# Hybrid decoder layer on one core: norm row spread by TensorE, zero products, later token tiles, one-part reload and paired weight groups

## The chip, the cores and the metric

The kernel runs on one core of one Trainium2 chip. The metric is device time in microseconds of one execution. A core has five engines that run their own instruction streams in order: TensorE (PE, with its weight loads listed apart as PEld), VectorE (DVE), ScalarE (ACT), GpSimd (POOL) and SyncE (SP), which here issues nearly all DMA transfers.

## The reference, cut to what matters

One decoder layer over 2048 tokens of width 1024. The input is RMS-normed once and multiplied by one input projection; its columns feed a gated DeltaNet (four heads, chunkwise) and a differential attention (four heads); both results are gated, concatenated, multiplied by an output projection and added to the input.

```python
def hybrid_mixer(layer_idx, x, cos, sin, w_norm, w_in, conv_w, ...):
    hn = rms_norm(x, w_norm)
    proj = jnp.einsum("bsd,de->bse", hn, w_in.astype(f32))
    q_a, k_a, v_a, z_a, b_a, a_a, q_b, k_b, v_b, z_b = jnp.split(proj, idx, axis=-1)
    qkv = jax.nn.silu(causal_depthwise_conv(jnp.concatenate([q_a, k_a, v_a], -1), conv_w))
    ...
    o_a = gated_delta_rule_chunked(q_a, k_a, v_a, g, beta)
    o_a = rms_norm(o_a, gdn_norm_w) * jax.nn.silu(z_a)
    ...
    o_b = diff_attention(q_b, k_b, v_b, lam)
    o_b = rms_norm(o_b, subln_w, SUBLN_EPS) * (1.0 - lam_init) * jax.nn.silu(z_b)
    return jnp.einsum("bse,ed->bsd", jnp.concatenate([o_a, o_b], -1), w_out)
```

## The kernel before

**Work.** Tokens are taken as 16 tiles of 128. A tile is loaded (`x_load`), squared and summed on ACT, scaled on DVE by its norm factor and by `wnb`, the norm weight spread over 128 partitions (`x_scale`), transposed on PE and split in two parts, `hh` and `hl`, by ACT and DVE (`x_split`). Four tiles make one instance of the pair (`hh`, `hl`), 512 tokens wide; only two instances fit in SBUF at a time.

**Input projection.** The columns of `w_in` are cut into groups of about 256; a group's weights come in two DMA halves (`wr`), are split into `wh` and `wl` (`w_stream`), and every product is three matmuls (wh·hh, wl·hh, wh·hl). There are three passes: pass 0 takes the first 1024 tokens through 8 groups (two gate groups, six DeltaNet groups), pass 1 the other 1024 tokens through all 16 groups, pass 2 the first 1024 tokens through the remaining 8. So instances 0 and 1 serve pass 0, 2 and 3 pass 1, 4 and 5 pass 2. The gate groups are token-major (256 or 264 moving columns, 24 matmuls for a tile), the DeltaNet groups channel-major (512 columns). `in_jobs` lists the jobs: inside a group the first 512 tokens (tb = 0), then the second (tb = 1); at a change of pass the last two groups are taken as a pair, both at tb = 0 and then both at tb = 1, so that the first instance comes free earlier.

**Reload.** Pass 2 needs the instances of pass 0 again. `hx_store` writes their `hh` and `hl` to DRAM, 8 transfers of 1 MB, and `hx_load` reads them back, 8 transfers of 1 MB.

**Order.** The instruction streams are written by a planner, `Flow`. Each part of the work is a generator that yields an engine, an earliest time and a condition; the planner always emits the piece that could start first by its own cost figures, ties broken by a priority. What it writes is then fixed: every engine runs its instructions in that order and waits on semaphores. SP issues its transfers in order too, and eight semaphore slots (`DMAHW0` to `DMAHW7`) are used in turn, so a transfer waits for the one eight places ahead.

**Places that the change touches.** `x_load` issues the tiles; after tile 0 it issues `wnb` as a broadcast read of `w_norm`. `consts` issues two parameter loads early and eleven more once eight tiles have been issued (`XC = 8`), and `w_stream` waits for eight tiles too before it issues the weights of the second group (`XW = 8`). `warm` runs 14 products of zeros on PE at the very start. `epilogue` takes finished products out of the three PSUM buffers `psi`; for gate groups ACT writes an `acc` tile, POOL multiplies it and SP stores it to `za_s`; there are three `acc` tiles. `gdn_a` prepares the DeltaNet blocks (`ssk`, `sv`, `sn`), `gdn_inv` joins the small triangular inverses through `z1`, `z2` and `Tn`.

## Time and profile before

| | us |
|---|---|
| three runs | 1499.89, 1502.4, 1511.44 |
| median of them | 1502.4 |
| the profiled execution | 1505.07 |
| its span, first to last instruction | 1503.3 |

| engine | busy us | share of the span |
|---|---|---|
| PE | 1447.9 | 96% |
| DVE | 954.0 | 63% |
| ACT | 844.4 | 56% |
| POOL | 708.3 | 47% |

The mean granted TensorE clock is 0.991 of its full 2.4 GHz. The profile is one execution. A row of a timeline has the start, the time from first start to last end, the engine, the source line, the operation with output and inputs, and in brackets the idle time before it and what ended it. Lines 81, 140, 152 and 165 are those of helpers that record every operation, so a row is told by its tiles. A matmul row's time contains its latency; successive starts give the rate. A windows row has the stretch, its length, the busy time of PE, PEld, DVE, ACT and POOL with instruction counts, then the granted clock, the DMA engines' busy share and GB/s.

### The profile page before, as it was taken

To read this page: it belongs to the slowest core of one execution; us is meant where nothing else is said; L and a number is where in the kernel's file an instruction comes from. 1 tells how busy PE (TensorE), PEld (TensorE's weight loads), DVE (VectorE), ACT (ScalarE), POOL (GpSimd) and SP (SyncE) were. 2 spreads that over 40 slices of the span, in tenths; PEclk is the share of its full clock that TensorE was granted. 3 is DMA by queue.
4 is the path that set the end of the run, shared out by engine and by line. 5 is a ranking of instruction groups with operands and counts; after the bars stand their busy time and mean duration, and the time that the engine had idled before them with its cause. 6 is when DMAs were issued, how large, how long until landed. Compare 5 with 4: busy or idle time off the path is not lost.

```text
span 1503.3 us, 28117 instructions
## 1 busy us (share of the span) xinstructions
PE 1447.9 (96%) x9959; PEld 1261.3 (84%) x9959; DVE 954.0 (63%) x2644; ACT 844.4 (56%) x1814; POOL 708.3 (47%) x662
## 2 busy tenths in 40 slices
PE   8899998999998999999999999999999999999998
PEld 6888888988778999998899899877887877888787
DVE  6466887569866667772554453217677777888852
ACT  5354464443565553224536543227777998988870
POOL 3411244600433645554452465625665676776661
PEclk9999999999999999999999999999999999999999
DMA  8665648464745665668766449247666454542425
GB/s 206 163 189 197 173 144 163 122 181 102 169 124 163 171 215 174 152 159 236 241 176 178 132 138 221 86 140 249 217 216 219 141 173 137 190 133 92 134 85 178
DMA packets 282893, 250.99 MB, mean 167 GB/s; under 512 B 47313, under 2 KB 252801, under 8 KB 280705
## 3 DMA queue, kind: packets, MB, share of 16 engines
q1 hardware_dynamic: 257408, 236.61, 55.3%
q10 hardware_dynamic: 25344, 12.59, 2.8%
q8 instruction: 79, 1.29, 0.3%
q14 instruction: 62, 0.50, 0.1%
HBM read 156.86 MB, written 92.27 MB: 166 GB/s over the span
## 4 chain that ended last, share of the span: by engine, by line
PE 74%; DMA 7%; DVE 6%; ACT 5%; POOL 4%; issue 2%; SPq 1%; ACTq 0%; POOLq 0%; DVEq 0%
PE psi L140 36%; PE psb L140 17%; PE pss L140 7%; PE psg L140 7%; PE psb L152 3%; ACT p L81 2%; PE psg L152 2%; PE tp L152 2%; DMA wr<-in_w_in_dram 1%; DMA qk_a<-gdx 1%; SPq L165 1%; POOL t L81 1%; DVE p L81 1%; DMA x<-in_x_dram 1%; DMA za_s<-acc 1%
## 5 line engine op out<-in xcount | busy, mean ns | idle before, releaser
L140 PE MATMUL psi<-wh,hh 128*128 128x256 f32 (+1 forms) x1024 | 305.3, 298 | 8.9 <-ACT acc L81 4.5
L140 PE MATMUL psi<-wl,hh 128*128 128x256 f32 (+1 forms) x1024 | 291.4, 285 | 1.3 <-DVE wl L81 1.3
L140 PE MATMUL psi<-wh,hl 128*128 128x256 f32 (+1 forms) x1024 | 290.9, 284 | 0.0
L81 DVE TENSOR_SCALAR_CACHE_REDUCE p<-pss 128x512 f32<-128x512 f32 (+3 forms) x320 | 179.4, 605 | 69.5 <-PE pss L140 66.6
L140 PE MATMUL psi<-hh,wh 128*128 128x512 f32 x512 | 205.8, 402 | 0.0
L140 PEld LDWEIGHTS psi<-wh,hh 128*128 128x128 f32 x1024 | 197.1, 192 | 10.4 <-ACT acc L81 4.9
L140 PE MATMUL psi<-hh,wl 128*128 128x512 f32 x512 | 202.1, 395 | 0.0
L140 PE MATMUL psi<-hl,wh 128*128 128x512 f32 x512 | 201.3, 393 | 0.0
L140 PEld LDWEIGHTS psi<-wl,hh 128*128 128x128 f32 x1024 | 197.4, 193 | 1.7 <-DVE wl L81 1.5
L140 PEld LDWEIGHTS psi<-wh,hl 128*128 128x128 f32 x1024 | 196.6, 192 | 0.0
L81 POOL TENSOR_TENSOR p<-p,p 128x640 f32<-128x640 f32 (+9 forms) x64 | 162.2, 2538 | 62.9 <-ACT p L81 58.1
L81 ACT ACTIVATE p<-p,nm 128x128 f32<-128x128 f32 (+15 forms) x128 | 153.2, 1200 | 20.8 <-DVE p L81 10.8
L81 ACT ACTIVATE raw<-psi 128x512 f32<-128x512 f32 (+1 forms) x96 | 57.2, 596 | 134.5 <-PE psi L140 113.7
L140 PE MATMUL psb<-th,v 128*128 128x256 f32 (+1 forms) x576 | 126.0, 293 | 1.5 <-DVE tl L81 1.2
L140 PE MATMUL pss<-kk,QQ 64*128 64x512 f32 (+3 forms) x960 | 123.2, 382 | 3.7 <-DVE p L81 1.8
L81 DVE SCALAR_TENSOR_TENSOR acc<-raw,cw,acc 128x512 f32<-128x512 f32 x144 | 112.3, 780 | 14.9 <-ACT acc L81 13.3
L81 ACT ACTIVATE p<-p,sc 128x128 f32<-128x128 f32 (+15 forms) x88 | 108.6, 1253 | 18.6 <-DVE sc L81 16.9
L140 PEld LDWEIGHTS psi<-hh,wl 128*128 128x128 f32 x512 | 96.0, 188 | 22.4
L81 DVE TENSOR_TENSOR tl<-psb,th 128x512 fp32r<-128x512 f32 (+2 forms) x176 | 92.9, 563 | 32.3 <-ACT th L81 30.7
L140 PEld LDWEIGHTS psi<-hl,wh 128*128 128x128 f32 x512 | 96.3, 188 | 20.1
L140 PEld LDWEIGHTS psi<-hh,wh 128*128 128x128 f32 x512 | 96.2, 188 | 19.7
L140 PEld LDWEIGHTS pss<-kk,QQ 64*128 64x128 f32 x960 | 80.3, 184 | 36.7 <-issue 9.3
(212 smaller groups left out, 3311.7 us busy)
## 6 DMA issues: line engine op xcount, KB each, us to landing
wr<-in_w_in_dram SPq DMA_DIRECT2D x80, 256.0 KB
x<-gdx SPq DMA_DIRECT2D x32, 512.0 KB
wr<-in_w_in_dram SPq DMA_DIRECT2D x24, 512.0 KB
gdx<-acc ACTq DMA_DIRECT2D x48, 256.0 KB
kk<-qk SPq DMA_DIRECT2D x48, 256.0 KB
v<-v SPq DMA_DIRECT2D x48, 256.0 KB
qk_a<-gdx SPq DMA_DIRECT2D x32, 256.0 KB
qk<-raw SPq DMA_DIRECT2D x32, 256.0 KB
```

The lines of the kernel that those rows point to most:

```text
L81: return call(*args, **kw)
L140: return self.nc.tensor.matmul(out=out, lhsT=lhsT, rhs=rhs, **kw)
L152: return self.nc.tensor.transpose(out=out, in_=in_, identity=identity)
L165: (self.nc.sync if by == "SP" else self.nc.scalar).dma_start(out=out, in_=in_, **kw)
```

## The change

- `w_norm` is loaded as one row of 1024 values; PE multiplies it by a row of ones (two f32 products of 512 columns), and DVE copies the two results to `wnb`.
- After the transposes of tile 0, 12 more products of zeros are issued on PE (`warm2`).
- Tiles 8 to 15 are issued only when three weight groups are done, and they may take one `x5` buffer fewer.
- In `in_jobs` the first two groups of every pass are paired as well, the first two of the program included.
- `hx_store` adds `hh` and `hl` on POOL into an `x5` tile and stores that (8 adds of 128x1024, 8 stores of 512 KB); `hx_load` loads it (4 loads of 1 MB) and splits it again: 4 copies on ACT and 4 subtractions on DVE, each of 128x2048.
- In `gdn_a` a negated `beta` is kept, so that `sn` comes from the reciprocal in one step; `sv` is computed on POOL afterwards.
- In `gdn_inv` the first copy into `z1` moves from ACT to DVE.

```diff
-    hx_s = [[dram.tile([P, KT, TB], F32, name=f"hx{i}_{j}") for j in range(2)] for i in range(2)]
+    hx_s = [dram.tile([P, KT, TB], F32, name=f"hx{i}") for i in range(2)]
...
+    wrow = ga.tile([1, D], F32, name="wrow", tag="fsX")
+    one = ga.tile([1, P], F32, name="one", tag="qk_a", bufs=2)
+    nc.vector.memset(one, 1.0)
+    def w_rows():
+        for i in range(2):
+            yield "PE", (lambda: t_row[0]), lambda: len(t_row) > 0, "+G"
+            ps = ps_g.tile([P, TB], F32, name="psg")
+            mm(out=ps, lhsT=one, rhs=wrow[:, i * TB:(i + 1) * TB], start=True, stop=True)
+            yield DV
+            wnb.append(wk.tile([P, TB], F32, name="wnb", tag=f"t1_{i}"))
+            dve.tensor_copy(out=wnb[i], in_=ps)
+            fl.release("G")
+            t_wn.append(fl.after("DVE"))
...
-                b = x_buf + ([(t_5[0], "ga")] if live5[0] < NX5 else [])
+                b = x_buf + ([(t_5[0], "ga")] if live5[0] < NX5 - (n > 7) else [])
...
-            yield "SP", (lambda: best()[0]), best
+            yield "SP", (lambda: best()[0]), lambda: best() if n < 8 or w_done[0] >= 3 else None
...
-                for i in range(2):
-                    wnb.append(wk.tile([P, TB], F32, name="wnb", tag=f"t1_{i}"))
-                    t_wn.append(dma(out=wnb[i], in_=bcast(w_norm)[:, i * TB:(i + 1) * TB]))
+                t_row.append(dma(out=wrow, in_=w_norm))
...
+    def warm2():
+        yield "PE", NOW, lambda: n_xt[0] > 1, "G"
+        ps = ps_g.tile([P, TB], F32, name="psg")
+        for _ in range(12):
+            fl.op("PE", 215)
+            nc.tensor.matmul(out=ps, lhsT=zw[0][:, :P], rhs=zw[0], start=True, stop=True)
...
-            for kh in range(2):
-                for j in range(2):
-                    yield "SP", NOW, lambda: w_done[0] >= HXW + 3 * (4 * i + 2 * kh + j) // 4
-                    t_hx[i] = dma(out=hx_s[i][j][:, kh * 4:kh * 4 + 4], in_=f(HX[i][j][:, kh * 4:kh * 4 + 4]))
+            for k in range(0, KT, 2):
+                yield "POOL", (lambda: max(*x_ready[i].values(), t_5[0])), (
+                    lambda: all((i, t) in x_done for t in range(4)) and live5[0] < NX5
+                    and w_done[0] >= HXW + 3 * (4 * i + k // 2) // 4)
+                live5[0] += 1
+                t = ga.tile([P, 2, TB], F32, name="x5", bufs=NX5)
+                pool.tensor_tensor(out=t, in0=f(HX[i][0][:, k:k + 2]), in1=f(HX[i][1][:, k:k + 2]), op=ALU.add)
+                yield SP
+                t_hx[i] = dma(out=hx_s[i][:, k:k + 2], in_=t)
...
+            for kh in range(2):
+                k4 = slice(kh * 4, kh * 4 + 4)
+                yield "ACT", (lambda: t_l[kh]), None
+                act.activation(hh[:, k4], hx[:, k4], AF.Copy)
+                yield DV
+                dve.tensor_tensor(out=r(hx[:, k4]), in0=hx[:, k4], in1=f(hh[:, k4]), op=ALU.subtract)
...
-        last = [gi for gi in range(len(groups) - 1) if groups[gi + 1][0] != groups[gi][0]] if SWAP else []
-        return sorted(jobs, key=lambda a: (a[0], 0) if a[0] not in last and a[0] + 1 not in last else
-                      (a[0] + (a[0] + 1 in last) - 1, a[1]))
+        new = [gi for gi in range(len(groups)) if gi == 0 or groups[gi - 1][0] != groups[gi][0]]
+        two = {}
+        for gi in new:
+            for g in (gi, gi - 2):
+                if g >= 0:
+                    two[g] = two[g + 1] = g
+        return sorted(jobs, key=lambda a: (two[a[0]], a[1]) if a[0] in two else (a[0], 0))
...
-            dve.reciprocal(out=sv, in_=ssk)
-            dve.tensor_tensor(out=sv, in0=sv, in1=st["beta"][:, h, cp], op=ALU.mult)
-            dve.tensor_scalar(out=sn, in0=sv, scalar1=-1.0, scalar2=None, op0=ALU.mult)
+            dve.reciprocal(out=sr, in_=ssk)
+            dve.tensor_tensor(out=sn, in0=sr, in1=st["nbeta"][:, h, cp], op=ALU.mult)
...
+            pool.tensor_tensor(out=sv, in0=sr, in1=st["beta"][:, h, cp], op=ALU.mult)
...
-                act.activation(z1[32:64, :, 0], ps[0:32, :, 0:32], AF.Copy)
...
+                dve.tensor_copy(out=z1[32:64, :, 0], in_=ps[0:32, :, 0:32])
```

The instruction order of three places follows. On TensorE, at the start of the kernel before: the last of the warm-up products (`fsT` holds zeros), the eight transposes of tile 0 (`x_180`), then the first products of the projection.

```order
L470 LDWEIGHTS fsT
L470 MATMUL psg<-fsT 128x512
L152 MATMUL tp<-ident,x_180 128x128 x8
L140 MATMUL psi<-wh,hh 128x256
L140 MATMUL psi<-wl,hh 128x256
L140 MATMUL psi<-wh,hl 128x256
```

The same place of the changed kernel, from the last warm-up product to the first of the new products of zeros; tile 0 is `x_183` here.

```order
L487 MATMUL psg<-fsT 128x512
L140 MATMUL psg<-wrow,one 128x512 x2
L152 MATMUL tp<-ident,x_183 128x128 x8
L495 LDWEIGHTS fsT
L495 MATMUL psg<-fsT 128x512
```

The two products that spread the norm row now stand ahead of the transposes, and twelve products of zeros stand behind them; the first projection product comes after those twelve and after four transposes of tile 1.

On TensorE, where the first group ends in the kernel before: `wh_226` and `wl_227` are the weights of the first group, `wh_478` those of the second, `hh_418` and `hl_419` the second instance (tiles 4 to 7), `hh_209` the first (tiles 0 to 3).

```order
L140 MATMUL psi_663<-wh_226,hh_418 128x256
L140 MATMUL psi_663<-wl_227,hh_418 128x256
L140 MATMUL psi_663<-wh_226,hl_419 128x256
L140 MATMUL psi_705<-wh_478,hh_209 128x264
L140 MATMUL psi_705<-wl_479,hh_209 128x264
```

The place in the changed kernel where the second group first appears: `wh_214` and `wl_215` are the first group's weights, `wh_549` and `wl_550` the second's, `hh_217` and `hl_218` the first instance, `x5_296` and `x5_348` tiles 6 and 7.

```order
L140 MATMUL psi_489<-wh_214,hh_217 128x256
L140 MATMUL psi_489<-wl_215,hh_217 128x256
L140 MATMUL psi_489<-wh_214,hl_218 128x256
L152 MATMUL tp_543<-ident_89,x5_296 128x128 x4
L152 MATMUL tp_552<-ident_89,x5_348 128x128 x4
L140 MATMUL psi_568<-wh_549,hh_217 128x264
L140 MATMUL psi_568<-wl_550,hh_217 128x264
L140 MATMUL psi_568<-wh_549,hl_218 128x264
```

The second group's weights are wanted after 96 products of the projection instead of after 192, while the tiles 4 to 7 are wanted only after 192 instead of after 96.

On SyncE, the transfers of the kernel before from tile 6 (`x_283`) and tile 7 (`x_317`) on: the four `wr` rows are the second group's weights, `xt` is tile 8, and the parameters begin with `dtb`.

```order
L165 DMA x_283<-in_x_dram 128x1024
L165 DMA x_317<-in_x_dram 128x1024
L165 DMA wr<-in_w_in_dram 128x4x256
L165 DMA wr<-in_w_in_dram 128x4x8
L165 DMA za_s<-acc_306 128x256
L165 DMA wr<-in_w_in_dram 128x4x256
L165 DMA wr<-in_w_in_dram 128x4x8
L165 DMA xt<-in_x_dram 128x1024
L165 DMA dtb<-in_dt_bias_dram 128x4
```

The end of the same stretch in the changed kernel, behind tile 7 and the first nine parameter loads; the `wr` rows are again the second group's weights.

```order
L165 DMA wqk<-in_q_norm_w_dram 128x64
L165 DMA wqk<-in_k_norm_w_dram 128x64
L348 DMA sub<-in_subln_w_dram 128x1
L165 DMA za_s<-acc_345 128x256
L165 DMA za_s<-acc_401 128x256
L165 DMA wr<-in_w_in_dram 128x4x256
L165 DMA wr<-in_w_in_dram 128x4x8
L165 DMA wr<-in_w_in_dram 128x4x256
L165 DMA wr<-in_w_in_dram 128x4x8
L165 DMA za_s<-acc_487 128x256
```

Eleven parameter loads and two stores now stand ahead of the second group's weights, which stood ahead of them before, and no tile from 8 on is issued in this stretch.

## Rows read from the trace of the kernel before

**Rows 1.** Windows by stage: start, pass 0, turn to pass 1, DeltaNet stretch.

```profile
0.00:79.20 79.20, 66.13 (x463) 60.33 (x464) 42.68 (x70) 35.95 (x87) 29.56 (x46) 0.91 0.71 179
79.20:195.00 115.80, 115.80 (x524) 94.87 (x523) 86.16 (x204) 55.77 (x87) 19.18 (x24) 1.00 0.62 183
195.00:330.00 135.00, 128.98 (x797) 114.92 (x797) 88.62 (x223) 70.98 (x127) 57.70 (x66) 0.97 0.62 156
330.00:900.00 570.00, 549.06 (x4244) 506.12 (x4243) 357.76 (x940) 272.52 (x822) 248.34 (x311) 1.00 0.62 168
...
sum 1503.30, PE 1447.94 PEld 1261.25 DVE 953.99 ACT 844.41 POOL 708.25; mean PE 206.85 PEld 180.18 DVE 136.28 ACT 120.63 POOL 101.18
```

**Rows 2.** Windows where the granted clock (third figure from the right) is low.

```profile
10.00:20.00 10.00, 7.01 (x33) 6.50 (x34) 7.66 (x10) 5.29 (x14) 2.62 (x5) 0.66 0.90 295
48.00:56.00 8.00, 8.00 (x49) 8.00 (x49) 6.71 (x15) 4.64 (x14) 6.31 (x9) 0.67 1.07 249
250.00:260.00 10.00, 7.28 (x40) 6.42 (x39) 5.38 (x17) 4.79 (x7) 5.96 (x8) 0.74 1.06 235
```

**Rows 3.** Waits of TensorE from 0 to 72 us: total, times, longest.

```profile
PE psi L140 <- ACT acc L81: 4.5, 2, 3.4
PE psi L140 <- DVE wh L81: 3.1, 1, 3.1
PE psi L140 <- DVE ab L81: 1.3, 1, 1.3
```

**Rows 4.** Timeline of TensorE, start of the kernel.

```profile
1.36 5.25 PE L470 MATMUL psg<-fsT 128*128 128x512 bf16 x14 [1.36 <-POOL fsT L467]
...
19.58 0.28 PE L140 MATMUL psi<-wh,hh 128*128 128x256 f32 x1
19.70 0.28 PE L140 MATMUL psi<-wl,hh 128*128 128x256 f32 x1
...
27.57 1.08 PE L152 MATMUL tp<-ident,xt 128*128 128x128 f32 x8
28.40 0.36 PE L140 MATMUL psi<-wh,hh 128*128 128x256 f32 x1
...
79.23 0.40 PE L140 MATMUL psi<-hh,wh 128*128 128x512 f32 x1
```

**Rows 5.** Timeline of SyncE's DMA issues, 21 to 42 us.

```profile
21.87 0.98 SPq L165 DMA_DIRECT2D wr<-in_w_in_dram  x2
...
28.66 3.25 SPq L165 DMA_DIRECT2D dtb<-in_dt_bias_dram  x1
...
40.20 1.96 SPq L165 DMA_DIRECT2D za_s<-acc  x3
```

**Rows 6.** Timeline of ScalarE, the longest wait of the start.

```profile
47.10 0.38 ACT L81 ACTIVATE acc<-psi 128x256 f32<-128x256 f32 x1 [5.73 <-DMA za_s<-acc]
```

**Rows 7.** Timeline of VectorE, start of the kernel.

```profile
6.11 1.41 DVE L81 SCALAR_TENSOR_TENSOR x<-x,rsx,wnb 128x512 f32<-128x512 f32 x2 [5.09 <-POOL rsx L81]
...
10.48 0.69 DVE L81 CAST wh<-wr 128x1024 fp32r<-128x1024 f32 x1 [1.55 <-DMA wr<-in_w_in_dram]
11.09 0.68 DVE L81 TENSOR_TENSOR hl<-tp,hh 128x512 fp32r<-128x512 f32 x1
11.69 1.21 DVE L81 TENSOR_TENSOR wl<-wr,wh 128x1024 fp32r<-128x1024 f32 x1
```

**Rows 8.** Timelines of POOL, VectorE and TensorE at the turn to pass 1.

```profile
243.78 2.48 POOL L81 TENSOR_TENSOR wl<-wr,wh 128x1056 fp32r<-128x1056 f32 x1 [0.94 <-ACT wh L81]
...
244.03 2.78 DVE L81 SCALAR_TENSOR_TENSOR x<-x,rsx,wnb 128x512 f32<-128x512 f32 x1
...
255.58 1.12 PE L152 MATMUL tp<-ident,x 128*128 128x128 f32 x4 [2.07 <-DVE hl L81]
```

**Rows 9.** Lines by shape: count, busy us, mean ns, idle before with its releasers.

```profile
L81 DVE TENSOR_TENSOR wl<-wr,wh 128x1024 fp32r<-128x1024 f32 x53 | 69.0, 1301 | 2.8 <-ACT wh L81 1.7
...
L81 ACT ACTIVATE wh<-wr 128x1024 fp32r<-128x1024 f32 x27 | 28.5, 1056 | 8.4 <-DMA wr<-in_w_in_dram 7.5 <-ACT acc L81 0.9
...
L81 POOL TENSOR_TENSOR wl<-wr,wh 128x1024 fp32r<-128x1024 f32 x7 | 17.4, 2489 | 20.1 <-ACT wh L81 20.1
```

More of the change, by code (lines that the diff above doesn't have):

```diff
@@ L433, in hybrid_kernel @@
     xq, x_buf = {}, [(0.0, "wk")] * NXB
+    t_row = []
+    wrow = ga.tile([1, D], F32, name="wrow", tag="fsX")
[11 more added lines that the diff above has]
+            t_wn.append(fl.after("DVE"))
     def x_load():
@@ L467, in warm @@
         nc.gpsimd.memset(z, 0.0)
+        zw.append(z)
         ps = ps_g.tile([P, TB], F32, name="psg")
@@ L470, in warm @@
             nc.tensor.matmul(out=ps, lhsT=z[:, :P], rhs=z, start=True, stop=True)
+    def warm2():
[4 more added lines that the diff above has]
+            nc.tensor.matmul(out=ps, lhsT=zw[0][:, :P], rhs=zw[0], start=True, stop=True)
     N_WARM = 14
+    zw = []
     def x_scale(par, of):
@@ L492, in x_scale @@
             for i in range(2):
-                yield "DVE", (lambda: max(t_r, t_wn[i])), None
+                yield "DVE", (lambda: max(t_r, t_wn[i])), lambda: len(t_wn) > i
                 hs = slice(i * TB, (i + 1) * TB)
@@ L535, in hx_store @@
         for i in range(2):
-            yield "SP", (lambda: max(x_ready[i].values())), lambda: all((i, t) in x_done for t in range(4))
-            for kh in range(2):
-                for j in range(2):
-                    yield "SP", NOW, lambda: w_done[0] >= HXW + 3 * (4 * i + 2 * kh + j) // 4
-                    t_hx[i] = dma(out=hx_s[i][j][:, kh * 4:kh * 4 + 4], in_=f(HX[i][j][:, kh * 4:kh * 4 + 4]))
+            for k in range(0, KT, 2):
[7 more added lines that the diff above has]
+                t_hx[i] = dma(out=hx_s[i][:, k:k + 2], in_=t)
+                live5[0] -= 1
+                t_5[0] = max(t_5[0], t_hx[i])
     t_hx = [0.0] * 2
@@ L548, in hx_load @@
             yield "SP", (lambda: max(t_xu[i + 2], t_hx[i])), lambda: x_used[i + 2]
-            hx = (hn.tile([P, KT, TB], F32, name="hh"), hn.tile([P, KT, TB], F32, name="hl"))
-            HX[i + 4] = tuple(r(h[:, :, :]) for h in hx)
+            hh = hn.tile([P, KT, TB], F32R, name="hh")
+            hx = hn.tile([P, KT, TB], F32, name="hl")
+            t_l = []
             for kh in range(2):
-                for j in range(2):
+                if kh:
                     yield "SP", NOW, None
-                    t = dma(out=hx[j][:, kh * 4:kh * 4 + 4], in_=hx_s[i][j][:, kh * 4:kh * 4 + 4])
+                t_l.append(dma(out=hx[:, kh * 4:kh * 4 + 4], in_=hx_s[i][:, kh * 4:kh * 4 + 4]))
+            for kh in range(2):
[4 more added lines that the diff above has]
+                dve.tensor_tensor(out=r(hx[:, k4]), in0=hx[:, k4], in1=f(hh[:, k4]), op=ALU.subtract)
                 if kh == 0:
-                    x_ready[i + 4] = {n: t for n in range(4)}
-                x_late[i + 4] = t
+                    x_ready[i + 4] = {n: fl.after("PE") for n in range(4)}
+                x_late[i + 4] = fl.after("PE")
+            HX[i + 4] = hh, r(hx[:, :, :])
             x_done.update((i + 4, n) for n in range(4))
@@ L816, in scalars @@
             dve.reciprocal(out=st["beta"], in_=t)
+            dve.tensor_scalar(out=st["nbeta"], in0=st["beta"], scalar1=-1.0, scalar2=None, op0=ALU.mult)
             yield "ACT", None, None
@@ L925, in gdn_a @@
             dve.tensor_scalar(out=ssk, in0=ssk, scalar1=EPS, scalar2=None, op0=ALU.add)
-            dve.reciprocal(out=sv, in_=ssk)
-            dve.tensor_tensor(out=sv, in0=sv, in1=st["beta"][:, h, cp], op=ALU.mult)
-            dve.tensor_scalar(out=sn, in0=sv, scalar1=-1.0, scalar2=None, op0=ALU.mult)
+            sr = ga.tile([P, 2], F32, name=f"sr{par}")
+            dve.reciprocal(out=sr, in_=ssk)
+            dve.tensor_tensor(out=sn, in0=sr, in1=st["nbeta"][:, h, cp], op=ALU.mult)
             yield "DVE", (lambda: t_e), None
@@ L1108, in gdn_inv @@
                 t_z2 = fl.after("PE")
-            if ua is not None:
-                act.activation(z1[32:64, :, 0], ps[0:32, :, 0:32], AF.Copy)
-                t_z1 = fl.after("PE")
             if ue is not None:
@@ L1116, in gdn_inv @@
             if ua is not None:
+                dve.tensor_copy(out=z1[32:64, :, 0], in_=ps[0:32, :, 0:32])
                 dve.tensor_copy(out=z1[96:128, :, 1], in_=ps[32:64, :, 0:32])
-                t_z1 = max(t_z1, fl.after("PE"))
+                t_z1 = fl.after("PE")
             if ub is not None:
@@ L1694, in hybrid_kernel @@
         fl.add(epilogue(par, NE), 0)
+    fl.add(warm2(), 0)
+    fl.add(w_rows(), 0)
     for gen in (q_load(), k_load(), out_x(), v_load()):
```

3 lines of the change are left out of this document (1 added, 2 removed).

## The prediction

> **What bounds the kernel now.** I read the windows by stage first. TensorE is busy 1447.9 of 1503.3 us [rows 1], so it is the bound nearly everywhere, and the change leaves its products as they are. It can only win back TensorE's idle time, 55.4 us in all, and the time lost to a lower clock. The reader is to see where the idle time lies: 13.1 us in the first 79.2 us, none in the rest of pass 0 (115.8 of 115.8 busy), 6.0 at the turn to pass 1, 20.9 in the 570 us in which the DeltaNet chain is woven into the projection [rows 1]. The remaining 15.4 us lie behind 900 us, in parts that the change does not edit.
>
> Second, the windows with a low clock [rows 2]. The granted clock is 0.66, 0.67 and 0.74 in three stretches of 8 to 10 us, which means that TensorE spent about 7 us of each at the lower of its two levels (1.2 GHz). Each such stretch costs about half of that, 3.4 us (0.34 x 10), and each stands during or just behind an idle time of TensorE. Over the first 79.2 us the clock is 0.91, so some 7 us are lost there besides the idle time.
>
> Third, the waits of the start [rows 3]. The two largest are 3.4 us for ACT to empty a `psi` buffer, and 3.1 us for the first `wh`. ACT in turn waited 5.73 us for an `acc` tile to be stored [rows 6], and SyncE tells why: the stores were issued at 40.20, behind parameter loads that began at 28.66 and crept forward for 11.5 us, since each waits for a slot that a 512 KB tile or weight transfer holds [rows 5]. So the middle of the start is bound by the transfer queue, the first 20 us by DVE and the first weights.
>
> **The change part by part.** Durations are those of the profiled execution, so the sum is made against its 1505.1 us, 1.8 more than its span and 2.7 above the median of the three runs.
>
> *Norm row by TensorE.* It removes 512 KB of transfer from in front of the first weights, which were awaited at 10.48 [rows 7], and adds work: two f32 products of 512 columns behind the warm-up, which ends at 6.6 (1.36 + 5.25) [rows 4]. One pass of 256 columns steps at 0.12 us [rows 4], so a pass of 512 takes 0.24 at least; bounds for the two products are 0.5 us at one pass each and some 2 us at several passes each. I take 1.7. DVE then gets its first operand about 7.6 instead of 6.11, and works in order through copy, scale, cast, copy, `wl`, `hl` and scale. By rows of the same width these are 0.7, 0.7, 0.7, 0.7, 1.2, 0.7 and 0.7 us [rows 7]: 5.4 us, so tile 0 is wholly scaled at about 13.0 and transposed at 13.4.
>
> *Zero products.* Twelve of them follow. The 14 of the warm-up took 5.25 us, 0.375 on average [rows 4]. TensorE idles some 3.5 us between 9.5 and 13 while DVE works, as it did in the kernel before ahead of 11.3 us, after which the clock fell [rows 2, 3]. So I price them at the lower clock, 0.43 us each, 5.2 us in all, which makes the first projection product start at 18.6; at the full clock, 0.21 each, it would be 16.0. In exchange what follows should run at full clock.
>
> *Later tiles and the paired first groups.* From 18.6 on TensorE has 384 gate products at 0.12 us, 46.1 us, and the transposes of seven tiles at 0.83 us (28.40 - 27.57) [rows 4], 5.8 us. It can do 96 products and six tiles of transposes, 16.5 us, before the second group begins, that is up to 35. The weights of the second group are issued later than before: then at 21.87 [rows 5], now behind tile 7 (which needs tile 2's buffer, about 22 to 23.5), eleven parameter loads at about 0.5 us each and two stores, so at 28 to 31. With two 512 KB halves, a cast and two subtractions at 1.3 us [rows 9] they are ready between 34 and 39. I take 2.5 us of waiting, bounds 0 and, if the small loads creep as they did before, 11. The wait of 3.4 us for the stores goes, and its 3.4 us of slow clock: tile 8 and those behind it are no longer in the queue, and TensorE can fill six jobs, 17 us (144 x 0.12), before the first store must have landed. Sum: 18.6 + 46.1 + 5.8 + 2.5 + 1 for small waits is 74.0, against 79.2 [rows 4]. The start gives 5 us. With the zero products at full clock and no wait it gives 11; with the second group's weights 10 us later it costs 5.
>
> *Paired groups at the turn.* When pass 1 begins, the first instance is now used for 192 products instead of 96, so TensorE needs tiles 12 to 15 11.5 us later (96 x 0.12). The wait for `hl` of 2.07 us [rows 8] should go, and with it part of the slow clock (0.74 over 10 us [rows 2], of which 2.6 us; the rest of the loss there is that idle time). Against it stands that DVE is the engine that is late there, and its load does not shrink. I take 3 us, bounds 7 and, through the POOL adds below, -2.5.
>
> *One-part reload.* It takes 4 MB of stores and 4 MB of loads away. It adds eight adds on POOL, about 2.49 us each [rows 9], 20 us. POOL is busy 19.2 of 115.8 us there [rows 1], so POOL itself hides them. DVE may not: a DVE scale that takes 0.7 us elsewhere took 2.78 and ended about 0.6 us behind the end of a POOL subtraction of two SBUF operands (243.78 + 2.48) [rows 8]. DVE has 29.6 us idle in pass 0 [rows 1], so I price this at nothing but for one add at the turn, 2.5 us at most. The load adds four copies on ACT, about 2.1 us each, and four subtractions on DVE, about 2.6 us each (twice the rows of 1024 columns [rows 9]). They lie at the turn to pass 2, in front of which TensorE has 96 products of 512 columns, 22 us, with the rest of the DeltaNet chain; a load of 1 MB, a copy and a subtraction fit into that twice.
>
> The Trainium skill (SBUF — State Buffer, SBUF: two separate sides) says that POOL and DVE share one port pair as an exclusive lock held for a whole instruction, the loser fully blocked. The row of 2.78 us agrees. By the rule alone all eight adds could block DVE, and with no slack on DVE the forecast would be 20 us later, near 1514; DVE's idle time in that stretch is why I weigh it at one add.
>
> *Shorter chain in `gdn_a`, join by DVE.* One small DVE instruction fewer in 32 blocks, 32 small copies moved to an engine that is 63% busy there (357.8 of 570 [rows 1]). The gain is what the idle time of 20.9 us allows and what a new order makes of it. I take 1 us, bounds 6 either way.
>
> Sum: 5 + 3 + 1 = 9 us, a profiled execution of 1496 and, 2.7 less, a median of 1494.
>
> **The rivals.** *All waits of the start and the turn clear.* The idle time and clock of both (13.1 + 7 and 6.0 + 3.4) would fall to the unavoidable first 10 us or so, and the gain is 11 + 7 + 2 = 20 us: 1482. For it speaks that each wait named has an edit aimed at it; against it that DVE, the late one at both places, only gets more work there.
>
> *The waits only move.* The planner writes a new order for 900 us, and TensorE runs it blindly; 20.9 us of idle time in the DeltaNet stretch [rows 1] show how far its figures are off. If start and turn give 8 and the new order takes as much, the median stays near 1501.
>
> *Slower: the second group's weights come late.* The place is TensorE's 97th product. If the eleven loads creep for 11.5 us as before [rows 5], the weights are ready near 46 and TensorE stands from 35, with 3.4 us of slow clock behind. Up to there the changed kernel is even until about 40. At 46 the start costs 5 us; with 1.5 lost at the turn and 2 to the rest, 8.5 us: 1511. Against it: fewer large transfers are in flight at that time.
>
> **How the numbers follow.** A measurement of this kernel can tell a change of about 1% from none, 15 us, that is 1487.4 and 1517.4. Forecast, 1488 to 1500: 0.45. All clear, about 1482: 0.27. Only moved, about 1501: 0.17. Slower, about 1511: 0.11. Faster by over 1% are nearly all of the second case and a fifth of the first, 0.35. Slower by over 1% is over half of the last, 0.07, for its price has no firm upper end. Within 1% is 0.58. The range takes the second case with 6 us more on one side and nearly all of the last on the other: 1476 to 1511.
>
> **What would show it.** First channel-major product near 74 instead of 79.2; a product every 0.12 us from about 19 on; no ACT wait on a store; TensorE's wait at the second group's first product 0 to 4 us. At the turn no wait for `hl` over 1 us and a clock of 1.0. POOL adds near 2.5 us. The prediction is wrong if the start does not shorten, if the clock falls again behind the second group, or if TensorE's idle time between 330 and 900 us moves by more than 6 us.

## The result and the profile after

The change makes the kernel slower by 0.7%: 1514.6 us (median of 9 runs, 1510.1 to 1521.6) against 1503.1 us for the kernel before in the same series (9 runs), ratio 1.0072 with a 95% interval of 1.0056 to 1.0088. The forecast was 1494, its range ended at 1511. The kernel before had medians from 1503.1 to 1508.4 us in the series that follow, so all comparisons below are ratios within one series. Stretches and milestones are from one profiled execution each.

Windows by stage of the kernel after, as in [rows 1], cut at its own first channel-major product (84.4 us):

```profile
0.00:84.40 84.40, 71.83 (x480) 61.56 (x481) 35.70 (x63) 30.04 (x67) 22.47 (x37) 0.88 0.52 124
84.40:195.00 110.60, 108.87 (x479) 88.04 (x477) 91.06 (x173) 60.11 (x100) 42.28 (x39) 0.98 0.57 169
195.00:330.00 135.00, 130.93 (x816) 116.63 (x817) 100.08 (x246) 71.23 (x129) 60.08 (x84) 0.99 0.66 165
330.00:900.00 570.00, 545.96 (x4163) 502.10 (x4162) 371.88 (x956) 280.44 (x804) 242.24 (x320) 0.99 0.61 160
```

The start is 5.2 us longer, not 5 shorter; TensorE's idle time in it is no larger (12.6 us against 13.1), its busy time is. Pass 0, which had no idle time of TensorE at all, now has 1.7 us of it up to 195 us and a clock of 0.98. The turn is better: 4.1 us idle instead of 6.0. The DeltaNet stretch is 3.1 us worse (24.0 idle against 20.9).

TensorE's idle time over the whole run hardly moved: 54.0 us (1514.3 - 1460.3) against 55.4. What grew is TensorE's *busy* time, by 12.3 us. The new products are 6.7 of it (4.74 for the zero products, 1.98 for the norm row); the rest, 5.6 us, goes with a lower clock. The windows with a low clock, as in [rows 2]:

```profile
9.00:19.00 10.00, 5.83 (x17) 2.94 (x18) 7.32 (x11) 4.09 (x10) 1.45 (x3) 0.50 0.83 289
40.00:50.00 10.00, 5.01 (x18) 4.20 (x19) 5.00 (x6) 1.08 (x1) 0.00 (x0) 0.65 0.94 128
267.00:274.00 7.00, 6.32 (x42) 6.31 (x42) 6.24 (x18) 2.91 (x5) 5.65 (x7) 0.76 0.22 35
660.00:670.00 10.00, 5.18 (x33) 5.18 (x34) 6.24 (x14) 0.60 (x1) 9.11 (x8) 0.66 0.69 209
780.00:790.00 10.00, 7.79 (x52) 7.33 (x52) 1.39 (x5) 3.34 (x12) 5.73 (x11) 0.66 0.57 168
```

Summed over windows of 5 us, as 5 x (1 - clock) and with the idle parts of those windows counted too, it is 27.2 us against 13.7 before. Each of these windows holds a wait or lies just behind one: 3.77 us up to 14.3, 5.0 us between 40 and 50, 4.8 between 660 and 670. Single waits of over 2 us add up to 20.3 us in the kernel after and to 14.9 in the kernel before. So much the same idle time, with more of it in long waits, goes with twice the slow clock; no run tests by itself whether the longer waits are the cause.

Waits of TensorE from 0 to 80 us, as in [rows 3]:

```profile
PE tp L152 <- DVE x L81: 4.7, 2, 3.8
PE psi L140 <- DVE wl L81: 2.7, 2, 2.0
PE psi L140 <- DVE wh L81: 2.2, 1, 2.2
```

The wait for ACT's `acc` of [rows 3] is gone. The waits for `wh` and `wl` are those for the second group's weights, in TensorE's timeline:

```profile
6.54 1.98 PE L140 MATMUL psg<-wrow,one 1*128 1x512 f32 x4
...
15.19 4.74 PE L495 MATMUL psg<-fsT 128*128 128x512 bf16 x12
...
20.12 0.36 PE L140 MATMUL psi<-wh,hh 128*128 128x256 f32 x1
...
41.37 0.39 PE L140 MATMUL psi<-wh,hh 128*128 128x264 f32 x1 [2.17 <-DVE wh L81]
43.74 0.59 PE L140 MATMUL psi<-wl,hh 128*128 128x264 f32 x1 [1.98 <-DVE wl L81]
47.46 0.59 PE L140 MATMUL psi<-wh,hh 128*128 128x264 f32 x1 [0.94 <-ACT wh L81]
...
48.75 0.59 PE L140 MATMUL psi<-wl,hh 128*128 128x264 f32 x1 [0.70 <-DVE wl L81]
```

Together TensorE waited 5.8 us for these weights.

SyncE's issues show where these weights stood, as in [rows 5], and VectorE's and ScalarE's timelines when they could be used:

```profile
25.32 0.70 SPq L165 DMA_DIRECT2D dtb<-in_dt_bias_dram  x1
...
30.34 0.43 SPq L348 DMA_DIRECT2D sub<-in_subln_w_dram  x1
30.87 0.85 SPq L165 DMA_DIRECT2D za_s<-acc  x2
31.77 4.31 SPq L165 DMA_DIRECT2D wr<-in_w_in_dram  x4
```

```profile
40.61 0.71 DVE L81 CAST wh<-wr 128x1056 fp32r<-128x1056 f32 x1 [2.11 <-DMA wr<-in_w_in_dram]
...
47.44 1.26 DVE L81 TENSOR_TENSOR wl<-wr,wh 128x1056 fp32r<-128x1056 f32 x1 [3.76 <-ACT wh L81]
```

```profile
46.33 1.08 ACT L81 ACTIVATE wh<-wr 128x1056 fp32r<-128x1056 f32 x1 [6.49 <-DMA wr<-in_w_in_dram]
```

The parameter loads did not creep (0.47 us each); the weights went out at 31.8 and still arrived only at 40.6 and 46.3 us. Between 40 and 50 us the DMA engines were 94% busy and moved 128 GB/s (windows above). The kernel before shows the same in two windows that the prediction did not read, with the same weights on the queue (issued from 21.87 on):

```profile
25.00:30.00 5.00, 5.00 (x44) 4.94 (x44) 4.10 (x8) 4.94 (x15) 3.99 (x6) 1.00 1.03 118
30.00:35.00 5.00, 4.42 (x39) 4.22 (x38) 5.00 (x8) 2.23 (x5) 2.75 (x4) 1.00 1.07 105
```

So the slow load (DMA engines full at 105 to 118 GB/s) is not new. New is that these weights are issued 10 us later and that TensorE wants them half a group sooner.

### The profile page after: what moved, and what is told of

It reads as the page before. It is cut to its first block, busy times and chain, and to the rows that moved or that the text cites. A ratio compares the mean times of both kernels' runs of the same rounds, so it can differ in the third digit from the quotient of the medians.

```text
span 1514.3 us, 28218 instructions
## 1 busy us (share of the span) xinstructions
PE 1460.3 (96%) x9975; PEld 1266.9 (84%) x9975; DVE 986.5 (65%) x2653; ACT 853.8 (56%) x1792; POOL 724.1 (48%) x698
## 4 chain that ended last, share of the span: by engine, by line
PE 75%; DVE 9%; DMA 6%; ACT 4%; POOL 3%; issue 2%; SPq 1%; ACTq 0%; DVEq 0%; POOLq 0%
PE psi L140 33%; PE psb L140 18%; PE psg L140 8%; PE pss L140 8%; PE psb L152 4%; DVE acc L81 2%; PE psg L152 2%; PE tp L152 2%; DMA x<-gdx 1%; DMA wr<-in_w_in_dram 1%; DVE wl L81 1%; DMA qk<-acc 1%; POOL rqx L81 1%; POOL t L81 1%; ACT acc L81 1%
## 5 line engine op out<-in xcount | busy, mean ns | idle before, releaser
L81 DVE SCALAR_TENSOR_TENSOR acc<-raw,cw,acc 128x512 f32<-128x512 f32 x144 | 116.1, 810 | 10.5 <-ACT acc L81 9.0
L81 ACT ACTIVATE p<-p,sc 128x384 f32<-128x384 f32 (+15 forms) x89 | 109.6, 1247 | 13.8 <-DVE sc L81 9.3
L140 PE MATMUL psb<-woh,oh 128*128 128x512 f32 x256 | 110.4, 431 | 0.7 <-DVE tl L81 0.6
```

Of the source, the lines that this page charges most:

```text
L81: return call(*args, **kw)
L140: return self.nc.tensor.matmul(out=out, lhsT=lhsT, rhs=rhs, **kw)
```

## The experiments

Sixteen kernels in four sets. "First" is the first channel-major product, "stretch" the time from there to the first product of pass 1. "Kept order" means that the planner counts what was taken out or moved as if it were still there, so that every instruction not named keeps its place; the others are planned anew. Milestones differ from one execution to the next: "after" and the two kept-order kernels that leave the start alone (no POOL adds, join's operand on ACT) have their first channel-major product between 83.0 and 84.7 us.

| kernel | first, us | stretch, us | ratio to before [95%] |
|---|---|---|---|
| before | 79.2 | 148.0 | 1 |
| after | 84.4 | 153.6 | 1.0072 [1.0056, 1.0088] |
| first two groups not paired | 79.3 | 154.9 | 0.9980 [0.9963, 0.9997] |
| second weights ahead of parameters | 84.9 | 154.5 | 1.0203 [1.0174, 1.0232] |
| parameters late | 77.8 | 163.1 | 1.0142 [1.0111, 1.0173] |
| old norm row, no zero products | 78.9 | 155.5 | 1.0023 [1.0006, 1.0040] |
| old reload | 84.0 | 147.5 | 0.9987 [0.9970, 1.0004] |
| planner's DVE constant, on after | 84.9 | 157.0 | 1.0286 [1.0254, 1.0318] |
| planner's DVE constant, on before | 80.9 | 148.0 | 1.0023 [1.0005, 1.0042] |
| planner's ACT constant, on before | 79.8 | 147.6 | 1.0044 [1.0028, 1.0059] |
| turn pairing alone, on before | 80.5 | 147.9 | 1.0153 [1.0123, 1.0182] |
| kept order: second weights first | 80.5 | 154.6 | 1.0043 [1.0028, 1.0058] |
| kept order: no zero products | 83.1 | 154.0 | 1.0065 [1.0048, 1.0082] |
| kept order: no POOL adds | 84.7 | 150.1 | 1.0017 [1.0003, 1.0031] |
| kept order: join's operand on ACT | 83.0 | 154.2 | 1.0077 [1.0055, 1.0099] |
| kept order, before: parameters late | 80.5 | 147.9 | 1.0017 [1.0003, 1.0031] |
| old reload + second weights first | 79.3 | 147.6 | 0.9967 [0.9948, 0.9987] |
| the same, stores between the halves | 78.2 | 147.3 | 0.9932 [0.9914, 0.9951] |

### The start

**First two groups not paired.**

```diff
-        new = [gi for gi in range(len(groups)) if gi == 0 or groups[gi - 1][0] != groups[gi][0]]
+        new = [gi for gi in range(1, len(groups)) if groups[gi - 1][0] != groups[gi][0]]
```

> The changed kernel, but the first two groups are not paired (the pairs at the turns stay). Theory A (the second group's weights come late, and pairing asks for them half a group too early): they are ready near 47 us as in the changed kernel, but are asked for only near 50, so TensorE's 5.0 us of idle time between 40 and 50 go, the first channel-major product comes near 79 instead of 84.4 us, and the median falls by about 5 us, to 1509 or 1510. Rival (the start is late because the zero products put the first projection product at 20 instead of 11 us): first channel-major product still at 83 us or later, median within 2 us of 1514.6. If the order that the planner writes behind it moves the time more than the start does, the median moves by another amount than the first channel-major product does.

The first channel-major product came at 79.3 us, 5.1 earlier, as theory A says. The ratio fell by more, 0.9%, although the POOL adds are still there (stretch 154.9): what lies beyond the start belongs to the new order and was not traced.

**Second group's weights ahead of the parameter loads**, planned anew.

```diff
-            yield "SP", NOW, lambda: n_xl[0] >= XC
+            yield "SP", NOW, lambda: n_xl[0] >= XC and n_w1[0] == 2
```

> The changed kernel with the second group's weights issued before the parameter loads instead of behind them; everything else stays. Theory A: issued at about 25 instead of 31.8 us, the weights are ready near 40, TensorE's idle time between 40 and 50 us falls from 5.0 to about 1, the first channel-major product comes near 79 to 80 us, and the median near 1510. Rival (the 32-byte packets of the gate columns make that load slow wherever it is issued, and the tiles are still under way): ready at 44 or later, first channel-major product at 83 us or later, median unchanged.

A miss. The weights were issued at 24.2 and their second half was cast at 39.2, but TensorE then waited 8.37 us all the same. VectorE's and ScalarE's timelines show what came instead: DVE stood for the last parameter, with the second `wl` behind it in its order, and ACT for a store.

```profile
46.08 0.15 DVE L81 TENSOR_SCALAR sub<-sub 128x1 f32<-128x1 f32 x1 [5.94 <-DMA sub<-in_subln_w_dram]
...
48.23 1.24 DVE L81 TENSOR_TENSOR wl<-wr,wh 128x1056 fp32r<-128x1056 f32 x1
```

```profile
46.43 0.38 ACT L81 ACTIVATE acc<-psi 128x256 f32<-128x256 f32 x1 [5.62 <-DMA za_s<-acc]
```

The start was hardly later than in the changed kernel (84.9 against 84.4), but the median 1.3% worse: that loss lies behind the start, in the new order, and was not traced further.

**Parameters late**, planned anew: the eleven loads and DVE's work on them wait until the first group is done.

```diff
-            yield "SP", NOW, lambda: n_xl[0] >= XC
+            yield "SP", NOW, lambda: n_xl[0] >= XC and w_done[0] >= 1
...
-        yield "DVE", (lambda: t_c + 2000), None
+        yield "DVE", (lambda: t_c + 8000), None
```

> The changed kernel with the eleven parameter loads, and the DVE work on them, put off until the first group's last product is planned; the second group's weights are then issued behind tile 7, and no parameter stands in front of them or of the first stores. The run with the weights moved alone showed them landed by 39 us, and DVE then standing 5.94 us for a parameter and ACT 5.62 us for a store, so the wait had only moved. Theory A: with both out of the way TensorE's idle time between 35 and 50 us falls from 5.0 to 1 or less, the first channel-major product comes near 78 to 79 us, and nothing of it is paid elsewhere. Theory of the order (behind the start, the time moves with each new order): the median is not 5 us below that of the changed kernel, but anything between 1500 and 1525. Rival: the paired start is late for another reason, first channel-major product at 83 or later.

First channel-major product at 77.8, 6.6 us earlier than after; the median is 0.7% worse than after all the same. Both theories held: the start is what theory A says, and the new order took more than it gave.

**The same move in the kept order.** SyncE's calls and DVE's calls on the parameters are put on lists while the planner counts them, and issued at a later place.

```diff
             t_c = dma(out=o, in_=i)
...
+                if gi == 1 and kh == 1:
+                    fl.flush(held[0])
...
+                if gi == 2 and kh == 0:
+                    fl.flush(held[1])
```

> The changed kernel with its order kept instruction for instruction on TensorE, ACT and POOL; only on SyncE the second group's weights go ahead of the eleven parameter loads and two stores, and DVE's eight instructions on the parameters come 9 to 11 places later. The planner does not see it, so nothing is ordered anew. Theory A with the theory of the order: the weights are issued near 25 instead of 31.8 us and ready near 40, TensorE's idle time between 35 and 50 us falls from 5.0 to 1 or less, the first channel-major product comes at 78 to 80 instead of 84.4 us, and since all behind it keeps its order the gain reaches the end: ratio to the kernel before 1.003 to 1.004 instead of 1.0072. The same two moves with a new order behind them gave 1.014. Rival (the pairing itself costs what the run without the pair saved, and a start that is 6 us earlier is lost in waits on DMA and POOL that stand at fixed times): ratio 1.006 or more.

First channel-major product 3.9 us earlier (80.5), and this time the gain lasts: pass 1 begins 2.9 us earlier, the projection ends 5.0 us earlier, the ratio is 1.0043. Of the wait 4.31 us stayed, behind an ACT that stood 2.67 us for a store. So the late weights cost about 4 us of the 11 (1.0072 - 1.0043 = 0.29%; with both intervals, 1 to 8 us).

**No zero products**, kept order.

```diff
-            nc.tensor.matmul(out=ps, lhsT=zw[0][:, :P], rhs=zw[0], start=True, stop=True)
```

> The changed kernel without the 12 zero products; the planner still counts them, so every other instruction keeps its place. If they only delay the first projection product: it comes at about 15.5 instead of 20.1 us, but the second group's weights are still ready only near 47, so TensorE waits longer for them and the first channel-major product stays at 83 to 84.4 us: ratio within 0.002 of 1.0072. If they keep the clock up for what follows (their purpose): the clock between 15 and 30 us falls below 1.0, and the first channel-major product is no earlier or later. If the start is bound by TensorE's own work: first channel-major product near 80, ratio 1.004.

First projection product at 15.8 instead of 20.1, first channel-major product at 83.1, which is within the spread of milestones, ratio unchanged: TensorE waits for the weights instead. The products delay nothing that counts as long as the weights are late. Nor do they raise the clock: from 15 to 30 us it was 0.88 without them and 0.86 with them.

**Old norm row, no zero products**, planned anew (the broadcast is two DMAs again, `w_rows` and `warm2` go).

> The changed kernel with the norm row broadcast by two DMAs as in the kernel before, and without the 12 zero products; the first two groups stay paired. (With these gone the planner also puts the second group's weights before the parameter loads.) If TensorE's broadcast and the zero products are what makes the start late: first projection product near 12 instead of 20.1 us, first channel-major product near 78, median near 1508. If only the late weights count: first channel-major product near 80 because the weights come earlier, and the idle time ahead of them is smaller. If both are harmless and the loss is further on: first channel-major product at 83 or later, median near 1514.

First projection product at 10.9, first channel-major product at 78.9. As the planner also put the weights ahead of the parameters, this alone does not tell the two apart.

**Parameters late in the kernel before**, kept order: SyncE's parameter loads behind three stores and three tiles.

> The kernel before with its order kept instruction for instruction on TensorE, ACT and POOL; on SyncE the eleven parameter loads go behind three stores and three tile loads, and DVE's eight instructions on the parameters come later. The 5.73 us that ACT waited for a store (and TensorE's 3.4 us for a psi buffer, with 1.6 us of slow clock behind) should go. If a gain at the start is kept when the order behind it is kept: first channel-major product near 75 instead of 79.2, ratio 0.997. If the waits behind the start stand at fixed times: first channel-major product early, ratio within 0.001 of 1.000.

A miss: the wait only moved. The third group's weights now stood behind the parameters (issued at 46.27), ACT's cast of them came after its longest wait, and TensorE lost 7.37 us behind it. First ScalarE's row, then TensorE's:

```profile
59.16 1.06 ACT L83 ACTIVATE wh<-wr 128x1024 fp32r<-128x1024 f32 x1 [11.41 <-DMA wr<-in_w_in_dram]
```

```profile
60.54 0.59 PE L143 MATMUL psi<-wh,hh 128*128 128x264 f32 x1 [7.37 <-ACT acc L83]
```

### The reload

**Old reload in two parts**, planned anew (hunk of `hx_store` and `hx_load` undone).

> The changed kernel with the old reload in two parts (both parts stored and loaded, no POOL adds, no copies and subtractions at the load). If the one-part reload is what costs behind the start: DVE's busy time between 100 and 200 us falls back from 83 to about 75 us, TensorE's waits there go, and the ratio to the kernel before falls from 1.007 to about 1.003 (the start's 5 us stay). If the reload is free, as forecast: ratio 1.007 within 0.002. If the order alone decides: ratio anywhere between 1.000 and 1.015, with the start still at 84.4 us, and waits of other names.

The stretch falls to 147.5 us, and the ratio from 1.0072 to 0.9987, although the start is still at 84.0. In the table every kernel with the two-part reload has a stretch of 147.3 to 148.0 us, whatever its order, and every one with the POOL adds 153.6 to 163.1. The windows of that stretch, of the kernel with the old reload and then of the kernel after:

```profile
84.00:231.50 147.50, 146.56 (x679) 120.28 (x678) 113.37 (x262) 84.43 (x144) 39.50 (x56) 1.00 0.65 201
```

```profile
84.40:238.00 153.60, 150.65 (x689) 122.34 (x688) 128.71 (x259) 85.89 (x147) 63.67 (x66) 0.99 0.58 167
```

DVE is busy 128.7 us with 259 instructions instead of 113.4 with 262. So single instructions have become longer; the next run shows which, and that it is the adds.

**No POOL adds**, kept order: SyncE stores the rounded part itself, and the second part is left out.

```diff
-                pool.tensor_tensor(out=t, in0=f(HX[i][0][:, k:k + 2]), in1=f(HX[i][1][:, k:k + 2]), op=ALU.add)
+                fl.op("POOL", 150 + 2.1 * 1024, [])
...
-                t_hx[i] = dma(out=hx_s[i][:, k:k + 2], in_=t)
+                t_hx[i] = dma(out=hx_s[i][:, k:k + 2], in_=f(HX[i][0][:, k:k + 2]))
```

> The changed kernel without the eight POOL adds of the reload: the rounded part alone is stored, the second part of the reloaded tokens is left out. The planner still counts the adds, so every other instruction keeps its place. Forecast (adds hidden): pass 0's channel-major stretch (84.4 to 238.0 us, 153.6 us against 148.0 before) is no shorter than 153, ratio within 0.002 of 1.0072. Rival (the adds hold up DVE or the psg buffers): that stretch falls by 3 us or more, the wait psg<-DVE tmp near 95 us goes, and the ratio falls to 1.005 or less.

The rival holds. The stretch is 3.5 us shorter, the last projection product comes 7.4 us earlier, and the ratio is 1.0017, so the eight adds cost 0.55% or 8 us (with both intervals, 5 to 11). The window of the stretch without them:

```profile
84.70:234.80 150.10, 148.28 (x689) 121.29 (x688) 117.28 (x259) 85.99 (x147) 45.37 (x58) 1.00 0.61 173
```

TensorE's and DVE's instructions are as many as with the adds, and DVE is busy 11.4 us less (117.3 against 128.7). The groups of DVE instructions in the stretch, with the adds and then without, show which were held up (busy us, mean ns):

```profile
L81 DVE TENSOR_TENSOR wl<-wr,wh 128x1024 fp32r<-128x1024 f32 x10 | 16.9, 1687 | 0.1
...
L81 DVE CAST wh<-wr 128x1024 fp32r<-128x1024 f32 x6 | 7.6, 1267 | 3.0 <-PE psi L140 1.9 <-DMA x<-in_x_dram 1.1
...
L81 DVE SCALAR_TENSOR_TENSOR x<-x,rsx,wnb 128x512 f32<-128x512 f32 x4 | 4.7, 1172 | 0.0
...
L81 DVE TENSOR_SCALAR ssk<-ssk 128x2 f32<-128x2 f32 x8 | 3.5, 442 | 0.0
```

```profile
L81 DVE TENSOR_TENSOR wl<-wr,wh 128x1024 fp32r<-128x1024 f32 x10 | 12.6, 1264 | 0.1
...
L81 DVE CAST wh<-wr 128x1024 fp32r<-128x1024 f32 x6 | 4.7, 782 | 3.9 <-PE psi L140 3.9
...
L81 DVE SCALAR_TENSOR_TENSOR x<-x,rsx,wnb 128x512 f32<-128x512 f32 x4 | 3.0, 744 | 0.0
L81 DVE TENSOR_SCALAR ssk<-ssk 128x2 f32<-128x2 f32 x8 | 1.3, 167 | 0.0
```

The wait that the rival named went as well. With the adds, TensorE waits 1.25 us for `tmp`, which DVE writes in the row of small instructions behind one that an add held up (the subtraction of 2.10 us shown further down), and its clock is low behind that wait; without the adds there is neither. TensorE's timeline and a window of the kernel after, then the window of the kernel without the adds:

```profile
95.54 0.41 PE L140 MATMUL psg<-tmp,le_blk 128*128 128x32 f32 x2 [1.25 <-DVE tmp L81]
```

```profile
94.00:104.00 10.00, 8.75 (x36) 6.97 (x35) 7.66 (x16) 6.83 (x12) 2.05 (x2) 0.83 0.38 101
```

```profile
92.00:104.00 12.00, 12.00 (x58) 9.86 (x57) 8.99 (x20) 8.52 (x14) 2.06 (x2) 1.00 0.46 136
```

The wait and the clock (10 x 0.17) make about 3 of the 3.5 us. The other 4 us up to the last projection product lie behind 238 us, where no add runs any more; where they come from was not traced.

### The turn and the join

**Turn pairing alone**, on the kernel before (the diff's `new` and `two`, without `gi == 0`).

> The kernel before with one edit alone: the jobs of the first two groups of each new pass are paired as well as the last two of the old one. Forecast: the waits of the turn to pass 1 (2.07 us for hl, idle time 6.0 us between 195 and 330, clock 0.74) get smaller, and the stretch from the first channel-major product of pass 0 to that of pass 1 is 3 us shorter than 211.9 us (79.2 to 291.1). In the changed kernel that stretch took 213.1 us (84.4 to 297.5), with the reload's work in it. Rival: the turn's gain is lost again in what follows, and the median stays within 3 us of the kernel before.

From one first channel-major product to the next it took 206.8 us (80.5 to 287.3) instead of 211.9: 5.1 us gained. This kernel is planned anew, and an order alone moves that stretch too: it took 211.6 us with the planner's DVE constant changed and 216.1 with the ACT constant. So the gain is clear in its direction, not in its size. The median is 1.5% worse: behind the turn pass 1's DeltaNet is woven in another way, and between 380 and 1000 us TensorE waits, among others, like this:

```profile
PE tp L152 <- POOL t L81: 15.3, 7, 6.2
PE psg L140 <- DMA comp<-d_s: 6.6, 2, 5.4
```

**Join's operand back on ACT**, kept order (the 32 copies of `z1`).

> The changed kernel with the 32 copies of the join's operand back on ACT; the planner still counts them as DVE's, so every other instruction keeps its place. Forecast of the prediction: this edit is worth 1 us either way in itself, ratio 1.006 to 1.008. Rival (DVE, the later engine, is what the join waits for): ratio 1.005 or less, TensorE's waits on DVE in the DeltaNet stretch smaller by 3 us or more.

No difference that can be measured, as forecast. The shorter chain in `gdn_a` was not tried by itself.

### The order alone

**Planner's constant for DVE**, 69 to 73 ns, on the kernel before; **for ACT**, 96 to 100, on the kernel before; and the first of them on the kernel after.

```diff
-                    ns = 69 + n * (0.52 if fast else 1.04) + (61 if ptr else 0)
+                    ns = 73 + n * (0.52 if fast else 1.04) + (61 if ptr else 0)
```

> The kernel before with one constant of the planner changed: it charges 73 instead of 69 ns for the fixed part of a DVE instruction. The program has the same instructions in another order. It sizes what a new order alone does. If the order matters as much as the change's edits (rival: the loss behind the start is scatter of the planner), the median moves by 3 to 12 us to either side of 1503 with the start unchanged, first channel-major product within 2 us of 79.2. If the order hardly matters, the median stays within 2 us of 1503, and the 6 us or so that the changed kernel loses behind its start must come from an edit.

> The kernel before with 100 instead of 96 ns for the fixed part of an ACT instruction on SBUF in the planner: the same instructions in another order. Theory of the order: ratio anywhere from 0.998 to 1.02, more likely above 1 than below, pass 0's channel-major stretch 148 us without an idle time as in all kernels with the two-part reload, the difference in the DeltaNet stretch behind it. Rival (a new order costs nothing when no instruction is added, and only the changed kernel is sensitive): ratio within 0.003 of 1.

> The changed kernel with 73 instead of 69 ns for the fixed part of a DVE instruction in the planner: the same instructions in another order. Theory of the order: the ratio to the kernel before differs from 1.0072 by 0.002 to 0.008 in either direction, the first channel-major product stays within 1 us of 84.4, and the difference lies in TensorE's idle time and lower clock between 84 and 1020 us. Rival (the loss behind the start belongs to the edits): ratio within 0.002 of 1.0072.

The same instructions in another order: 0.2% and 0.4% slower than before, and 2.1% slower than after (1.0286 / 1.0072). In the last one TensorE waits 10.0 us for weights between 330 and 900 us, and never for that in the same stretch of the kernels before and after. The size, 2.1%, was more than the 0.8% that I had allowed for.

### Both causes undone

**Old reload, second group's weights first**, in the order of the run with the old reload; and the same **with the two stores between the halves of the weights**.

```diff
-                if gi == 1 and kh == 1:
+                if gi == 1 and kh == 0:
                     fl.flush(held[0])
```

> The run with the old reload (ratio 0.9987), its order kept, with the second group's weights ahead of the parameter loads and two stores as in the run that moved the weights in the kept order. If the two causes add up and account for the loss: first channel-major product near 80 instead of 84.0, and the gain of 0.3% reaches the end: ratio 0.995 to 0.997, faster than both kernels. If the run with the old reload was a lucky order, in which the start's loss was covered later: ratio 0.998 or more.

> As the run before it in this set, but the two stores go between the two halves of the second group's weights instead of behind them, so that ACT does not wait 2.67 us for a store ahead of its cast. If that wait holds the second half's cast: first channel-major product 1 to 2 us earlier than in that run, ratio 0.001 lower. If the transfers themselves are late: no difference, ratio within 0.001.

First channel-major product at 79.3 and 78.2 us, ratios 0.9967 and 0.9932: faster than both kernels. The wait for the weights is down to 2.23 us, in TensorE's timeline of the last one:

```profile
41.66 0.39 PE L143 MATMUL psi<-wl,hh 128*128 128x264 f32 x1 [2.23 <-DVE wl L83]
```

The second step, 1.1 us at the start, came out 0.35% faster; the two intervals just overlap, so how much of it is real is open. Against the kernel before the last one is 0.7% faster.

## Why the prediction was wrong

(The prediction's sum, 1496 less 2.7, is 1493, not 1494; nothing hangs on it.)

**The start, forecast -5, was +5.2.** The 12 zero products took 4.74 us (forecast 5.2), the norm row 1.98 (1.7); the first projection product came 1.5 us late, at 20.1 (forecast 18.6). The step that failed is "I take 2.5 us of waiting". The weights were issued at 31.8, little behind the 28 to 31 that I had worked out, but I gave the transfer, cast and subtractions 6 to 8 us; they took almost 17 (31.77 to 47.44 + 1.26). TensorE waited 5.8 us for them. The slow clock behind the wait has no term in the sum at all: between 40 and 50 us it is 3.5 us, idle parts counted in. The slower rival named place and time, "ready near 46", and priced it at 5 us, with the wrong cause: the loads did not creep. Moving the weights in the kept order gave 4 us back.

**The reload, forecast 0, costs about 8 us.** The step that failed is "I price this at nothing but for one add at the turn". DVE's idle time in pass 0 is an average. The adds fall on the casts and subtractions of weights, on tiles, and on small instructions ahead of the DeltaNet blocks, and TensorE waits for one of these (the 1.25 us above). In the timelines of the kernel after, POOL and then VectorE:

```profile
87.31 2.85 POOL L81 TENSOR_TENSOR x<-hh,hl 128x1024 f32<-128x1024 f32 x1
...
110.39 2.40 POOL L81 TENSOR_TENSOR x<-hh,hl 128x1024 f32<-128x1024 f32 x1
```

```profile
88.08 2.10 DVE L830 TENSOR_TENSOR negl<-le__135 128x1 f32<-128x1 f32 x1 [0.18 <-ACT le__135 L81]
90.22 0.15 DVE L831 TENSOR_SCALAR negl<-negl 128x1 f32<-128x1 f32 x1
...
111.04 2.30 DVE L81 CAST wh<-wr 128x1024 fp32r<-128x1024 f32 x1 [1.13 <-DMA x<-in_x_dram]
```

A subtraction of one element per partition took 2.10 us and ended at 90.18, 0.02 behind the add (87.31 + 2.85 = 90.16). Without the adds the same subtraction took 0.16 us. The row of 2.10 us agrees with the rule of the Trainium skill that the prediction weighed (SBUF — State Buffer, SBUF: two separate sides), that the loser of the shared port waits for the whole instruction. My "by the rule alone" sum of 20 us was too high, one add at the turn far too low: the adds, 18.3 us of POOL time in the stretch (63.67 - 45.37), made DVE's work there 11.4 us longer. Each add took 2.4 to 2.9 us, as forecast.

**The turn, forecast -3 (bounds -7 to +2.5), was right in its direction:** 5.1 us in a kernel of its own order, and in the changed kernel an idle time there of 4.1 instead of 6.0. In its own kernel the gain did not reach the end, since the same edit sends all that follows into another order.

**The chain and the join, forecast -1.** The join on DVE changes nothing measurable.

**The new order, "6 either way", was too narrow.** Three changes of a planner's constant, with no instruction added, cost 0.2, 0.4 and 2.1%, that is 3 to 32 us. All three cost time. The single edits that were planned anew moved as far: the early weights by +1.3% against after with the start unmoved, the turn alone by +1.5% with the turn gained. The four kernels in the changed kernel's kept order moved by 0.55% at most, and the two that gained show where.

**What it adds up to.** In the kept order the weights are worth 0.29% and the adds 0.55%; 1.0072 less both is 0.9988, so the two account for the loss. The intervals of the three ratios leave that difference open by some 0.3% either way. Both undone in one kernel gave 0.9967, in an order of its own. What is left to the turn, the chain and the order of the changed kernel is thus within the intervals and can't be divided further.

## What to carry to other kernels

Where a planner writes the order, measure an edit with the order kept (count the old cost, issue the new work), for a new order alone moved this kernel by up to 2%. An add on POOL is not free because POOL and DVE have idle time on average: look for the small DVE instructions that TensorE waits for and that would stand behind it. When groups are paired so that each tile is used twice, the second group's weights are due after half as many products, and everything ahead of them on their queue, and behind them on the engines that cast them, must be looked at again.

## What was not expected

- A DVE instruction of one element per partition took 2.10 us beside a POOL add, and one of two columns 442 ns on average instead of 167.
- A half of the second group's weights (128x1056 f32, 528 KB, its gate columns in runs of 32 bytes) took 9 to 13 us from issue to cast, and the DMA engines were 94% busy between 40 and 50 us at only 128 GB/s. By the packet records of the trace the 32-byte packets themselves filled only 3 to 5% of the engines' time from 35 to 50 us, so why the load is slow stays open.
- The idle time fell by 1.3 us while the sum for the lower clock doubled (13.7 to 27.2): how idle time is spread seems to count, not only how much there is. No run tests this by itself.
